# A new order for the first part of a decoder step, with four smaller edits in it

## The chip, the cores and the metric

The kernel runs on one core of one Trainium2 chip. The metric is the device time of one execution in microseconds (us). The profile describes one execution; the runs beside it are timed without it.

The engines are named as in the profile: PE (matrix engine), DVE (vector engine), ACT (scalar engine), POOL, and SP, which here only issues transfers (DMA). SBUF is the on-chip memory with 128 partitions, PSUM the small memory that PE writes into.

## What is computed

One layer of a decoder for 288 tokens: one prompt of 256, and 8 sequences with 4 new tokens each (the sample part, 32 tokens). Cut to what matters:

```python
z = rms_norm(x) @ w_in                      # 1024 -> u, va, q, k, vb, 512 each
u = gelu(u); va = rms_norm(gelu(va)); q = rms_norm(q); k = rms_norm(k)   # per head or group
# (A) gate, 4 groups of 128: within chunks of 128 tokens (prompt) or 4 (sample)
a = u * (tril(a_ws) @ va + a_bs)
# (B) attention, 8 heads of 64. Prompt: causal over 256 tokens. Sample: 8 pages of 128 past tokens
#     per sequence through a page table; of the four blocks of 256 past tokens a query keeps the
#     best three by q . mean(k), and always its own new tokens
o = softmax(q k^T / 8, selected) @ v
h = x + concat(a, o) @ w_out
h = h + relu(rms_norm(h) @ w_up)**2 @ w_down
h = h + ple_norm-scaled((sigmoid(rms_norm(h) @ w_ple_gate)) * (p @ w_ple_proj))
```

New k and v, and va of the sample part, are outputs too.

## The kernel before

Features lie on the partitions, tokens along the free dimension (N = 288). Every projection is done as high and low part: a weight chunk of 128 x 1024 (`raw`, 512 KB, four buffers) is split by ACT into `hi` (L124) and by DVE into `lo = raw - hi` (L129), three buffers each, and PE runs three matmuls for each 128 x 128 piece (`mm3`, L236 to L238). There are 98 such chunks, c0 to c97. A whole chunk is 24 matmuls of 288 columns. `split` (L242 to L246) makes the high and low part of an activation.

The first part, up to the output projection, is run by the string `ORDER`, one letter for a step; `w_up`, `w_down` and the last gate follow in loops. The letters: `r` first norm and the query projections c0 to c3 that are done beside it; `w` the next weight unit: key projections k0 to k3 (c4 to c7), values v0 to v3 (c8 to c11), the gate's va a0 to a3 (c12 to c15), u0 to u3 (c16 to c19), output projections out0.0 to out0.3 and out1.0 to out1.3; `E` one of the two chunks for the per-layer input (c24, c29); `T` the next tile of the page cache, K0 to K7 for keys, V8 to V15 for values, the first four of each for one half of the sequences, the last four for the other; `A` prompt attention for one pair of heads (A0 to A3); `G` the gate for one group (G0 to G3); `l` loads the gate's tables `aws`, `abd`, `abs` on ACT's queue, `m` masks them on DVE; `P` loads the per-layer input `pT` on ACT's queue; `s`, `S` store outputs. A unit is a generator: it issues its PE work at its place, and hands on the rest (`yield`) to be resumed some steps later.

PE and SP run in the order in which the program is written. ACT and DVE instructions are placed by a scheduler that looks at what each waits for. So what a PE step waits for depends on where its ACT and DVE steps came to stand.

PSUM: three buffers `mm` (projections), three `misc` (norm statistics, transposes, prompt scores, gates, new keys' scores, own values), two `S` (page scores and the weighted sum of values). Each prompt attention takes two `misc` buffers for its scores, each gate one.

A key tile (`u_K`, L556) is 16 matmuls of 32 query columns by 256 keys in four column tiles of the array. After the fourth tile of a half come the scores of the new keys (L564): four matmuls of 128 x 32 into `po`. DVE then works out which blocks each query keeps (L573 to L591), and ACT the exponentials (L594, L596). They are transposed into `PT`, and `u_V` multiplies: first the new values (L628), then eight matmuls of 512 columns for each value tile (L635). When the fourth value tile is in, DVE masks the sum per head (`Om`), and four matmuls with the constant `sel` (L650) bring the own value of each head into rows of features.

The statistic of a norm is a matmul with a block of ones (`stat`, L227 as `misc<-tmp`), then `rsqrt_act` (ACT: L256 reciprocal root y, L257 -x/2, L258 y squared) and `rsqrt_dve` (DVE: L262, L263), which is a Newton step.

Transfers: the 16 first-part tiles T are 8 pages of 256 KB each, issued by SP into four buffers, in order. Chunks c6 to c31 (`W_POOL` = 32) are issued from POOL's queue, all others by SP in line with the pages. The semaphores of transfers from SP's and ACT's queues are eight, taken in turn; a page whose turn comes on one that an earlier ACT transfer holds waits until that has landed.

Of the kernel before, what the change touches and what calls it, by code (L numbers as in the profile page):

```python
# [10 lines left out]
AF = mybir.ActivationFunctionType  # L11
# [14 lines left out]
NWARM = 8  # L26
NV = 38
NPOOL = 80
W_POOL = 32

ORDER = (
    "r w w w l w T w w T w w T w T w T w w m w T w w T w T A G T A G G T G s A A w T T P w T T w w T T S E w w w w E"
).split()

PLE = [4 + i for i, t in enumerate([t for t in ORDER if t in "wE"]) if t == "E"]
# [3 lines left out]
def tile_decode_step(ctx: ExitStack, tc: tile.TileContext, w, xT, pT, kT, vP, pt, const, aws, abd, abs_,  # L42
# [29 lines left out]
    pt_sb = stile([1, 64], "pt", dt=I32)  # L72
    cst = stile([128, 732], "const")
    aws_sb = stile([128, 4, 128], "aws")
    abd_sb = stile([NS, 4, NS], "abd")
    abs_sb = stile([128, 4, 128], "abs")

    gx = stile([128, NV + 8 * N], "h")
    vec_sb = gx[:, :NV]
    h = gx[:, NV:].rearrange("p (k n) -> p k n", k=8)  # L80
    ones = stile([128, 128], "ones")
    eps = stile([128, 1], "eps")
    pool.dma_start(pt_sb, pt)
# [37 lines left out]
    def split_hi(c, a=0, b=1024):  # L121
        if a == 0:
            hi[c] = stile([128, 1024], "hi", NHI, F32R)
        act.activation(hi[c][:, a:b], raw[c][:, a:b], AF.Copy)  # L124
# [105 lines left out]
    def tr(out, src, us=0.11):  # L230
        pe.transpose(out, src, ident)  # L231
        cur["pe"] += us
# [12 lines left out]
            act.activation(dh, src, AF.Copy, scale=scale)  # L245
            dve.scalar_tensor_tensor(dl, src, scale, dh.bitcast(F32), OP.mult, OP.subtract)  # L246

    def stat(src, lhsT):
        p = misc_ps()
        mm(p[:, :N], lhsT, src, 0.49, start=True, stop=True)  # L250
        return p[:, :N]

    def rsqrt_act(ss, count):

        y, v, y2 = tmp(), tmp(), tmp()
        act.activation(y, ss, AF.Abs_reciprocal_sqrt, bias=eps, scale=1.0 / count)  # L256
        act.activation(v, ss, AF.Identity, bias=heps, scale=-0.5 / count)  # L257
        act.activation(y2, y, AF.Square)  # L258
        return y, v, y2

    def rsqrt_dve(r, y, v, y2):
        dve.tensor_tensor(v, v, y2, OP.mult)  # L262
        dve.scalar_tensor_tensor(r, v, 1.5, y, OP.add, OP.mult)  # L263

    def g_rstd(name, acc):
        t = rsqrt_act(stat(acc, ones), D)
        yield 0
        st[name] = stile([128, N], "rs", 2)
        rsqrt_dve(st[name], *t)
# [15 lines left out]
    act.dma_start(gx[:, 0:NV + N], xT[:, 0:NV + N])  # L285
    load_x(act, 1, 2)
    first = stile([128, 1], "first")
    act.activation(first, eps, AF.Abs_reciprocal_sqrt)
    for c in range(1, 4):
        load_x(sp, 2 * c, 2 * c + 2)  # L290
        load_w(c, 2)
# [88 lines left out]
    def u_qk(c, name, tag, g):  # L380
        p = qp[c][:, :N] if c < 4 else k8(c, Ah, Al, misc_ps() if c == 5 else None)
        yield 1
        j, dst = in_tile(c, name, tag)
        dve.tensor_tensor(dst, p, st["r1"], OP.mult)
        sq = tmp()
        act.activation(sq, dst, AF.Square)
        yield (3.3 if c < 2 else 6.4 if c < 4 else 6,)
        t = rsqrt_act(stat(sq, blk), 64)
        yield 0
        r = tmp()  # L390
        rsqrt_dve(r, *t)
        dve.scalar_tensor_tensor(dst, dst, g, r, OP.mult, OP.mult)  # L392
        finish(name)
        if name == "q":
            for hh in range(2):
                pp = slice(64 * hh, 64 * hh + 64)
# [28 lines left out]
    def u_a(c):  # L425
        p = k8(c, Ah, Al)
        yield 1
        j, dst = in_tile(c, "a", "T1")
        dve.tensor_tensor(dst, p, st["r1"], OP.mult)
        act.activation(dst, dst, AF.Gelu_apprx_tanh)  # L430
        sq = early[:, 384 * j:384 * j + N]
        act.activation(sq, dst, AF.Square)
        st[f"sq{j}"] = sq
        if j < 3:
            return
        for i in range(2):
            yield (2.5,)
            ts = [rsqrt_act(stat(st[f"sq{j}"], ones), 128) for j in (2 * i, 2 * i + 1)]
            yield 0
            for j in (2 * i, 2 * i + 1):  # L440
                r = tmp()
                rsqrt_dve(r, *ts[j % 2])
                dst = st["a"][:, j]
                dve.scalar_tensor_tensor(dst, dst, avn(j), r, OP.mult, OP.mult)
        for j in range(4):
            if j % 2 == 0:
                yield (3.0,)
            t = early[:, 384 * j:384 * j + 384]
# [18 lines left out]
    def u_g(g):  # L467
        need(("u", 4), ("a", 4))
        an = st[f"an{g}"]
        p = misc_ps()  # L470
        cur["pe"] += 1.0
        for c in range(2):
            pe.matmul(p[:, 128 * c:128 * c + 128], lhsT=an[:, 128 * c:128 * c + 128], rhs=aws_sb[:, g, :],
                      start=True, stop=True)
        pe.matmul(p[:, NP:N], lhsT=an[0:NS, 256:384], rhs=abd_sb[:, g, :], start=True, stop=True)
        yield 1
        Mh, Ml = mix()
        t = tmp()
        dve.tensor_tensor(t[:, :NP].rearrange("p (c t) -> p c t", c=2), p[:, :NP].rearrange("p (c t) -> p c t", c=2),
                          abs_sb[:, g:g + 1, :].to_broadcast([128, 2, 128]), OP.add)  # L480
        dve.tensor_tensor(t[:, NP:].rearrange("p (b t) -> p b t", b=8), p[:, NP:N].rearrange("p (b t) -> p b t", b=8),
                          abs_sb[:, g:g + 1, 0:4].to_broadcast([128, 8, 4]), OP.add)
        dve.tensor_tensor(t, t, st["u"][:, g], OP.mult)
        act.activation(Mh[:, g], t, AF.Copy)
        yield 0
        dve.tensor_tensor(Ml[:, g], t, Mh[:, g].bitcast(F32), OP.subtract)
        finish("g")
# [57 lines left out]
    def u_K(t):  # L545
# [14 lines left out]
        if n == 3:  # L560
            need(("k", 4))
            po = misc_ps()
            for j in range(4):
                pe.matmul(po[:, 0:NS], lhsT=Qbd[:, 256 * j + 128 * g:256 * j + 128 * g + 128],  # L564
                          rhs=st["k"][:, j, NP:N], start=j == 0, stop=j == 3)
        cur["used"] += 1
        yield 1
        if n == 0:
# [51 lines left out]
    def u_V(t):  # L620
        g, n = t // 4 - 2, t % 4
        need((f"PT{g}", 1), ("v", 4))
        cur["pe"] += 1.9
        PT, vt = st[f"PT{g}"], kvt[t]
        if n == 0:
            st["O"] = s_ps()
            for b in range(4):
                pe.matmul(st["O"][32 * b:32 * b + 32, :], lhsT=PT[0:NS, 1024 + 32 * b:1056 + 32 * b], rhs=vn_s,  # L628
                          start=True, stop=False, tile_position=(0, 32 * b))
        O = st["O"]  # L630
        for j in range(2):
            for b in range(4):
                c = 128 * (2 * n + j) + 32 * b
                v0 = 512 * (2 * b + j)
                pe.matmul(O[32 * b:32 * b + 32, :], lhsT=PT[:, c:c + 32], rhs=vt[:, v0:v0 + 512],  # L635
                          start=False, stop=n == 3 and j == 1, tile_position=(0, 32 * b))
        cur["used"] += 1
        if n < 3:
            return
        finish(f"V{g}")  # L640
        yield 1
        Om = stile([128, 4 * N], "T4")[:, :512] if g else early[:, 0:512]
        dve.scalar_tensor_tensor(Om.rearrange("p (h d) -> p h d", h=8), O.rearrange("p (h d) -> p h d", h=8),
                                 st[f"rs{g}"], hmask[:, :, None].to_broadcast([128, 8, 64]), OP.mult, OP.mult)
        yield (1.6,)
        Mh, Ml = mix()
        p = misc_ps()
        cur["pe"] += 0.9
        for j in range(4):
            pe.matmul(p[:, 16 * j:16 * j + 16], lhsT=Om[:, 128 * j:128 * j + 128], rhs=sel, start=True, stop=True)  # L650
# [36 lines left out]

    def mask_aws():
        dve.tensor_tensor(aws_sb, aws_sb, tri[:, None, :].to_broadcast([128, 4, 128]), OP.mult)
# [211 lines left out]
```

## Time and profile before

| | us |
|---|---|
| median of 3 runs (lowest, highest) | 411.98 (411.09, 412.75) |
| profiled execution | 410.52 |
| its span in the profile | 408.8 |
| PE busy in it | 397.0 (97%) |
| DVE, ACT, POOL busy | 267.7, 211.1, 15.6 |
| mean granted clock of PE | 0.990 of full speed |

The span is what the profile's lines add up to; the execution is 1.7 us longer. A line of a timeline gives start, duration, engine, line of the code, operation, what it writes and reads, its shape, how many instructions of the kind stand together, and in brackets how long the engine was idle before and what ended that. Busy times of PE overlap a little, since its instructions are pipelined: the difference of two starts says better how long a group holds PE. In a list of waits stand the total, the number and the longest.

### The profile page before, as it was taken

The numbers are of one execution on the slowest core, as the hardware profiler recorded it, in microseconds if no ns is written. First come the engines' busy times: TensorE is split into PE (matmuls) and PEld (weight loads), VectorE is DVE, ScalarE is ACT, GpSimd is POOL, SyncE is SP. The second block draws the span as 40 slices with busy tenths as digits, with TensorE's granted clock in tenths as the row PEclk, the third lists the DMA queues.
The fourth block names the chain that finished last, engine by engine and source line by source line (L and its number), as shares of the span: only waits on it lengthen the run. The fifth ranks groups of instructions, "written<-read, shape, count | busy, mean of one in ns | idle before, by whom it ended". The sixth has DMA issues, their size and how long they took to land.

```text
span 408.8 us, 8115 instructions
## 1 busy us (share of the span) xinstructions
PE 397.0 (97%) x3082; PEld 364.0 (89%) x3082; DVE 267.7 (65%) x514; ACT 211.1 (52%) x377; POOL 15.6 (4%) x32
## 2 busy tenths in 40 slices
PE   8989999999799999999999999999999999999995
PEld 7978887987255679999999999999999999999994
DVE  4878765566587344969989778874454445544773
ACT  7677738588455225866554454444433343333630
POOL 1210110111000010000000000000000000000000
PEclk9999999999699999999999999999999999999999
DMA  8999899999949972444444454445444545444411
GB/s 283 402 396 353 311 398 393 391 391 388 372 132 313 396 283 101 156 162 179 176 156 156 164 179 173 156 156 170 180 163 157 162 170 185 154 157 171 154 54 49
DMA packets 37270, 92.39 MB, mean 226 GB/s; under 512 B 4656, under 2 KB 6096, under 8 KB 37232
## 3 DMA queue, kind: packets, MB, share of 16 engines
q1 hardware_dynamic: 32688, 77.10, 52.9%
q0 software_dynamic: 3776, 13.63, 8.7%
q10 hardware_dynamic: 768, 1.15, 0.9%
q8 instruction: 24, 0.39, 0.4%
q14 instruction: 14, 0.11, 0.1%
HBM read 89.44 MB, written 2.42 MB: 225 GB/s over the span
## 4 chain that ended last, share of the span: by engine, by line
PE 84%; DMA 5%; DVE 5%; ACT 3%; issue 2%; SPq 0%; DVEq 0%; POOLq 0%; ACTq 0%
PE mm L236 24%; PE mm L238 24%; PE mm L237 23%; PE S L635 4%; DMA raw<-w 3%; PE S L556 3%; PE misc L227 2%; PE misc L231 2%; DMA aws<-aws 1%; DVE lo L129 1%; DMA h<-xT 1%; ACT hi L124 1%; PE S L628 1%; DVE T L392 1%; DVE tmp L263 1%
## 5 line engine op out<-in xcount | busy, mean ns | idle before, releaser
L124 ACT ACTIVATE hi<-raw 128x1024 fp32r<-128x1024 f32 (+2 forms) x107 | 108.8, 1018 | 144.4 <-PE mm L237 123.2
L129 DVE TENSOR_TENSOR lo<-raw,hi 128x1024 fp32r<-128x1024 f32 (+2 forms) x107 | 125.4, 1173 | 64.0 <-ACT hi L124 62.2
L236 PE MATMUL mm<-T,hi 128*128 128x288 f32 x296 | 88.1, 298 | 0.0
L238 PE MATMUL mm<-T,lo 128*128 128x288 f32 x296 | 87.2, 294 | 0.0
L237 PE MATMUL mm<-T,hi 128*128 128x288 f32 x296 | 86.4, 292 | 0.0
L236 PE MATMUL mm<-Ah,hi 128*128 128x288 f32 x264 | 80.4, 305 | 0.0
L237 PE MATMUL mm<-Al,hi 128*128 128x288 f32 x264 | 77.9, 295 | 0.0
L238 PE MATMUL mm<-Ah,lo 128*128 128x288 f32 x264 | 77.7, 294 | 0.0
L236 PE MATMUL mm<-kv,hi 128*128 128x288 f32 x224 | 66.1, 295 | 0.0
L237 PE MATMUL mm<-kv,hi 128*128 128x288 f32 x224 | 66.0, 295 | 0.0
L238 PE MATMUL mm<-kv,lo 128*128 128x288 f32 x224 | 65.9, 294 | 0.0
L237 PEld LDWEIGHTS mm<-T,hi 128*128 128x128 f32 x296 | 55.7, 188 | 0.1
L236 PEld LDWEIGHTS mm<-T,hi 128*128 128x128 f32 x296 | 55.6, 188 | 0.1
L238 PEld LDWEIGHTS mm<-T,lo 128*128 128x128 f32 x296 | 55.4, 187 | 0.0
L236 PEld LDWEIGHTS mm<-Ah,hi 128*128 128x128 f32 x264 | 49.5, 188 | 2.8 <-issue 2.4
L237 PEld LDWEIGHTS mm<-Al,hi 128*128 128x128 f32 x264 | 49.6, 188 | 0.4
L238 PEld LDWEIGHTS mm<-Ah,lo 128*128 128x128 f32 x264 | 49.7, 188 | 0.0
L237 PEld LDWEIGHTS mm<-kv,hi 128*128 128x128 f32 x224 | 42.3, 189 | 0.0
L238 PEld LDWEIGHTS mm<-kv,lo 128*128 128x128 f32 x224 | 42.2, 189 | 0.0
L236 PEld LDWEIGHTS mm<-kv,hi 128*128 128x128 f32 x224 | 42.0, 188 | 0.0
L759 DVE TENSOR_TENSOR tmp<-mm,rs 128x288 f32<-128x288 f32 x32 | 14.6, 456 | 11.0 <-PE mm L238 10.9
L119 POOL DMA_DIRECT2D raw<-w x26 | 13.7, 529 | 143.6 <-DVE lo L129 143.6
(170 smaller groups left out, 432.9 us busy)
## 6 DMA issues: line engine op xcount, KB each, us to landing
raw<-w SPq DMA_DIRECT2D x72, 512.0 KB, 3.2
kv<-kT SPq DMA_DIRECT2D x64, 256.0 KB, 7.5
kv<-vP SPq DMA_DIRECT2D x64, 256.0 KB, 6.5
raw<-w POOLq DMA_DIRECT2D x26, 512.0 KB, 6.5
raw<-w SPq DMA_DIRECT2D x8, 256.0 KB, 4.9
y_o<-h SPq DMA_DIRECT2D x7, 144.0 KB, 1.8
h<-xT SPq DMA_DIRECT2D x3, 288.0 KB, 5.2
k_o<-T SPq DMA_DIRECT2D x1, 576.0 KB, 7.3
```

Source lines behind the costliest of these rows:

```text
L119: (pool if 6 <= c < W_POOL else sp).dma_start(raw[c][:, n * i:n * i + n], w[c][:, n * i:n * i + n])
L124: act.activation(hi[c][:, a:b], raw[c][:, a:b], AF.Copy)
L129: dve.tensor_tensor(lo[c][:, a:b], raw[c][:, a:b], hi[c][:, a:b].bitcast(F32), OP.subtract)
L227: pe.matmul(out, lhsT=lhsT, rhs=rhs, **kw)
L231: pe.transpose(out, src, ident)
L236: pe.matmul(out, lhsT=wh, rhs=xh, start=start, stop=False)
L237: pe.matmul(out, lhsT=wh, rhs=xl, start=False, stop=False)
L238: pe.matmul(out, lhsT=wl, rhs=xh, start=False, stop=stop)
L263: dve.scalar_tensor_tensor(r, v, 1.5, y, OP.add, OP.mult)
L556: pe.matmul(S[32 * b:32 * b + 32, c0:c0 + 256].rearrange("p (j s) -> p j s", j=2), lhsT=Qbd[:, q0:q0 + 32], rhs=kt[:, b, :, j, :], start=j ...
L635: pe.matmul(O[32 * b:32 * b + 32, :], lhsT=PT[:, c:c + 32], rhs=vt[:, v0:v0 + 512], start=False, stop=n == 3 and j == 1, tile_position=(0, ...
L759: dve.tensor_tensor(t, p, st["r2"], OP.mult)
```

## The change

It is five edits in one.

The order of the first part. With names in place of letters, before:

```
r k0 k1 k2 l k3 K0 v0 v1 K1 v2 v3 K2 a0 K3 a1 K4 a2 a3 m u0 K5 u1 u2 K6 u3 K7 A0 G0 V8 A1 G1 G2 V9 G3
s A2 A3 out0.0 V10 V11 P out0.1 V12 V13 out0.2 out0.3 V14 V15 S E(c24) out1.0-1.3 E(c29)
```

and after:

```
r k0 k1 k2 k3 v0 l v1 v2 K0 v3 a0 K1 K2 a1 m K3 a2 A0 K4 a3 u0 K5 K6 u1 u2 u3 K7 A1 G0 A2 G1 P G2 G3
V8 V9 A3 out0.0 V10 V11 out0.1 s V12 V13 out0.2 V14 out0.3 V15 S E(c24) out1.0-1.3 E(c29)
```

With it `W_POOL` goes from 32 to 26, so c26 to c31 are issued by SP: c26 behind V13's pages, the others behind V15's.

Shorter norms: for the first two model-wide norms and the four query norms the ACT step L257 goes, and the first of the two DVE steps now reads the statistic from PSUM; the model-wide norm's Square on ACT is put ahead of the split of c6 there. The fourth query statistic is written to an `S` buffer in place of `misc`. The new keys' scores become 16 matmuls of 32 x 32, in four column tiles. The own values become four transposes and a sum on DVE over 128 x 512 to 128 x 64. The gate's sample part multiplies over all 128 rows in place of 32, with `abd` padded by zeros from 16 to 64 KB and four POOL clears of 128 x 128.

```diff
-W_POOL = 32
+W_POOL = 26
 ORDER = (
-    "r w w w l w T w w T w w T w T w T w w m w T w w T w T A G T A G G T G s A A w T T P w T T w w T T S E w w w w E"
+    "r w w w w w l w w T w w T T w m T w A T w w T T w w w T A G A G P G G T T A w T T w s T T w T w T S E w w w w E"
...
-    abd_sb = stile([NS, 4, NS], "abd")
+    abd_sb = stile([128, 4, NS], "abd")
...
-        act.activation(hi[c][:, a:b], raw[c][:, a:b], AF.Copy)
+        i = act.activation(hi[c][:, a:b], raw[c][:, a:b], AF.Copy)
+        if c == 6:
+            after(i, st["r1_act"])
...
-    def rsqrt_act(ss, count):
+    def rsqrt_act(ss, count, short=False):
...
+        if short:
+            half, a = {1024: (1, 4), 64: (1, 2)}[count]
+            act.activation(y, ss, AF.Abs_reciprocal_sqrt, bias=eps[:, half:half + 1], scale=4.0 ** half / count)
+            st["r1_act"] = act.activation(y2, y, AF.Square, scale=2.0 ** -a)
+            dve.scalar_tensor_tensor(y2, ss, count * EPS, y2, OP.add, OP.mult)
+            return y, 1.5 * 2 ** half, y2
...
+        if isinstance(v, float):
+            dve.scalar_tensor_tensor(r, y2, v, y, OP.subtract, OP.mult, reverse0=True)
+            return
...
-        t = rsqrt_act(stat(acc, ones), D)
+        t = rsqrt_act(stat(acc, ones), D, True)
...
-        t = rsqrt_act(stat(sq, blk), 64)
+        t = rsqrt_act(stat(sq, blk, s_ps() if c == 3 else None), 64, c < 4)
...
+            pool.memset(t[:, 256:384], 0.0)
...
-        pe.matmul(p[:, NP:N], lhsT=an[0:NS, 256:384], rhs=abd_sb[:, g, :], start=True, stop=True)
+        pe.matmul(p[:, NP:N], lhsT=an[:, 256:384], rhs=abd_sb[:, g, :], start=True, stop=True)
...
-                pe.matmul(po[:, 0:NS], lhsT=Qbd[:, 256 * j + 128 * g:256 * j + 128 * g + 128],
-                          rhs=st["k"][:, j, NP:N], start=j == 0, stop=j == 3)
+                for b in range(4):
+                    q0 = 256 * j + 128 * g + 32 * b
+                    pe.matmul(po[32 * b:32 * b + 32, 0:NS], lhsT=Qbd[:, q0:q0 + 32], rhs=st["k"][:, j, NP:N],
+                              start=j == 0, stop=j == 3, tile_position=(0, 32 * b))
...
-            pe.matmul(p[:, 16 * j:16 * j + 16], lhsT=Om[:, 128 * j:128 * j + 128], rhs=sel, start=True, stop=True)
-        yield 1
+            tr(p[:, 128 * j:128 * j + 128], Om[:, 128 * j:128 * j + 128])
+        yield 1
+        o = tmp()[:, :64]
+        dve.tensor_reduce(o, p.rearrange("p (t h) -> p t h", h=8), AX.X, OP.add)
```

What moves on the engines, at two places. First DVE at the first norm. `lo_437` and `lo_436` are the low part of c5, `lo_439` and `lo_438` that of c6, `rs` the norm's scale, and the last row the first use of it. Before:

```order
27 L129 TENSOR_TENSOR lo_437<-raw_263,hi_395 128x1024
28 L129 TENSOR_TENSOR lo_439<-raw_265,hi_397 128x1024
29 L262 TENSOR_TENSOR tmp_383<-tmp_383,tmp_384 128x288
30 L263 SCALAR_TENSOR_TENSOR rs_388<-tmp_383,tmp_382 128x288
31 L384 TENSOR_TENSOR T_54_399<-S_111,rs_388 128x288
```

After:

```order
28 L137 TENSOR_TENSOR lo_436<-raw_264,hi_394 128x1024
29 L269 SCALAR_TENSOR_TENSOR tmp_384<-misc_381,tmp_384 128x288
30 L278 SCALAR_TENSOR_TENSOR rs_388<-tmp_384,tmp_383 128x288
31 L137 TENSOR_TENSOR lo_438<-raw_266,hi_396 128x1024
32 L402 TENSOR_TENSOR T_53_398<-S_112,rs_388 128x288
```

The norm's two steps now stand between c5's and c6's low parts, no longer behind both.

Second PE from key tile K7 (first row of each) to value tile V8 (last). L564 and L585 are the new keys' scores; L227 and L235 with `T,T` operands the scores of a prompt attention (A0 before; A1, then A2 after); L473, L475 and L492, L494 a gate; L628 and L649 the new values. Before:

```order
522 L556 MATMUL S_1435<-kv_1027,T_11_75 32x256 x16
523 L564 MATMUL misc_1560<-T_66_449,T_11_75 128x32 x4
524 L227 MATMUL misc_1596<-T_66_449,T_54_399 128x128
525 L227 MATMUL misc_1597<-T_66_449,T_54_399 128x128
526 L227 MATMUL misc_1596<-T_66_449,T_54_399 128x256
527 L227 MATMUL misc_1597<-T_66_449,T_54_399 128x256
528 L473 MATMUL misc_1618<-aws_63,e_74 128x128 x2
529 L475 MATMUL misc_1618<-abd_64,e_74 128x32
530 L628 MATMUL S_1634<-vns_379,PT_1198 32x512 x4
531 L635 MATMUL S_1634<-kv_1112,PT_1198 32x512 x8
```

After, from the end of G0 (rows 532 to 538 are the same steps as 522 to 528 before, for A1 and with 16 matmuls at L585):

```order
539 L494 MATMUL misc_1680<-abd_64,e_75 128x32
540 L235 MATMUL misc_1694<-T_65_448,T_53_398 128x128
541 L235 MATMUL misc_1695<-T_65_448,T_53_398 128x128
542 L235 MATMUL misc_1694<-T_65_448,T_53_398 128x256
543 L235 MATMUL misc_1695<-T_65_448,T_53_398 128x256
544 L492 MATMUL misc_1714<-aws_63,e_75 128x128 x2
545 L494 MATMUL misc_1714<-abd_64,e_75 128x32
546 L492 MATMUL misc_1734<-aws_63,e_75 128x128 x2
547 L494 MATMUL misc_1734<-abd_64,e_75 128x32
548 L492 MATMUL misc_1744<-aws_63,e_75 128x128 x2
549 L494 MATMUL misc_1744<-abd_64,e_75 128x32
550 L649 MATMUL S_1754<-vns_380,PT_1227 32x512 x4
```

Four more steps, A2 and three gates, now stand between G0 and the first value matmuls; A0 has gone ahead of K7.

More of the change, by code (lines that the diff above doesn't have):

```diff
@@ L81, in tile_decode_step @@
     ones = stile([128, 128], "ones")
-    eps = stile([128, 1], "eps")
+    eps = stile([128, 2], "eps")
     pool.dma_start(pt_sb, pt)
     dve.memset(ones, 1.0)
-    dve.memset(eps, EPS)
+    dve.memset(eps[:, 0:1], EPS)
+    dve.memset(eps[:, 1:2], 4 * EPS)
     heps = stile([128, 1], "heps")
@@ L123, in split_hi, with after @@
             hi[c] = stile([128, 1024], "hi", NHI, F32R)
-        act.activation(hi[c][:, a:b], raw[c][:, a:b], AF.Copy)
+        i = act.activation(hi[c][:, a:b], raw[c][:, a:b], AF.Copy)
+        if c == 6:
+            after(i, st["r1_act"])
+    def after(late, early):
+        tc.add_manual_dep(late.ins, early.ins.name, mybir.DependencyInfo(
+            mybir.DependencyClass.NoSync, mybir.DependencyReason.DATA), reason="after")
     def split_lo(c, a=0, b=1024):
@@ L246, in split, with stat @@
             dve.scalar_tensor_tensor(dl, src, scale, dh.bitcast(F32), OP.mult, OP.subtract)
-    def stat(src, lhsT):
-        p = misc_ps()
+    def stat(src, lhsT, p=None):
+        p = misc_ps() if p is None else p
         mm(p[:, :N], lhsT, src, 0.49, start=True, stop=True)
         return p[:, :N]
-    def rsqrt_act(ss, count):
-        y, v, y2 = tmp(), tmp(), tmp()
-        act.activation(y, ss, AF.Abs_reciprocal_sqrt, bias=eps, scale=1.0 / count)
+    def rsqrt_act(ss, count, short=False):
+        y, v, y2 = tmp(), None if short else tmp(), tmp()
+        if short:
[4 more added lines that the diff above has]
+            return y, 1.5 * 2 ** half, y2
+        act.activation(y, ss, AF.Abs_reciprocal_sqrt, bias=eps[:, 0:1], scale=1.0 / count)
         act.activation(v, ss, AF.Identity, bias=heps, scale=-0.5 / count)
@@ L287, in tile_decode_step @@
     first = stile([128, 1], "first")
-    act.activation(first, eps, AF.Abs_reciprocal_sqrt)
+    act.activation(first, eps[:, 0:1], AF.Abs_reciprocal_sqrt)
     for c in range(1, 4):
@@ L647, in u_V @@
         p = misc_ps()
-        cur["pe"] += 0.9
         for j in range(4):
-            pe.matmul(p[:, 16 * j:16 * j + 16], lhsT=Om[:, 128 * j:128 * j + 128], rhs=sel, start=True, stop=True)
+            tr(p[:, 128 * j:128 * j + 128], Om[:, 128 * j:128 * j + 128])
         yield 1
+        o = tmp()[:, :64]
+        dve.tensor_reduce(o, p.rearrange("p (t h) -> p t h", h=8), AX.X, OP.add)
         tk = slice(NP + 16 * g, NP + 16 * g + 16)
-        split(Mh[:, 4:8, tk], Ml[:, 4:8, tk], p[:, 0:64].rearrange("p (j t) -> p j t", j=4))
+        split(Mh[:, 4:8, tk], Ml[:, 4:8, tk], o.rearrange("p (j t) -> p j t", j=4))
         finish("O")
@@ L689, in mask_aws @@
         dve.tensor_tensor(aws_sb, aws_sb, tri[:, None, :].to_broadcast([128, 4, 128]), OP.mult)
-        dve.tensor_tensor(abd_sb, abd_sb, tri[0:NS, None, 0:NS].to_broadcast([NS, 4, NS]), OP.mult)
+        dve.tensor_tensor(abd_sb, abd_sb, tri[:, None, 0:NS].to_broadcast([128, 4, NS]), OP.mult)
     in_units = (
@@ L883 @@
         "pt": A(page_table).reshape(1, 64), "const": _constants(),
-        "aws": aws, "abd": abd.reshape(NS, 4, NS), "abs": A(a_bs)[0],
+        "aws": aws, "abd": np.concatenate([abd.reshape(NS, 4, NS), np.zeros((96, 4, NS), np.float32)]), "abs": A(a_bs)[0],
     }
```

## The prediction

> **What bounds the kernel now.** I read the page first, then windows cut at the places the change touches, then waits, timelines and the chain there.
>
> ```profile
> span 408.8 us, 8115 instructions
> PE 84%; DMA 5%; DVE 5%; ACT 3%; issue 2%; SPq 0%; DVEq 0%; POOLq 0%; ACTq 0%
> ```
>
> PE is the bound: the chain of work that ended last is 84% PE, the rest scattered. The granted clock dips once. So a change is worth what it takes out of PE's work or gaps. Windows (window, length, busy PE, PEld, DVE, ACT, POOL, granted clock, DMA share, GB/s):
>
> ```profile
> 30.00:99.95 69.95, 69.66 (x652) 59.52 (x650) 46.65 (x98) 49.81 (x100) 7.38 (x14) 1.00 1.01 375
> 99.95:105.03 5.08, 2.91 (x27) 2.30 (x23) 4.05 (x24) 2.05 (x6) 0.53 (x1) 0.88 1.05 392
> 105.03:110.60 5.57, 5.57 (x26) 0.93 (x26) 1.88 (x8) 3.23 (x15) 0.00 (x0) 0.50 1.03 387
> 110.60:121.60 11.00, 10.24 (x78) 6.33 (x78) 8.40 (x37) 5.03 (x18) 0.00 (x0) 1.00 0.48 164
> 121.60:152.97 31.37, 31.33 (x256) 20.35 (x254) 16.65 (x42) 10.46 (x25) 2.11 (x4) 1.00 0.90 325
> 180.00:260.00 80.00, 80.00 (x605) 79.89 (x604) 70.12 (x123) 40.90 (x63) 0.00 (x0) 1.00 0.47 164
> ```
>
> 99.95 is the end of key tile K7 and 152.97 the start of chunk c24: 53.0 us with a hole, a stretch at half clock (5.57 us at 0.50, and 0.12 x 5.08 / 0.5 = 1.2 us before it) and small waits. From there on PE streams without a gap, as in the last row: what is won earlier is not taken back.
>
> **Part by part.** *Short norms, c6's order, fourth statistic in another PSUM tag.*
>
> ```profile
> 19.09 0.65 PE L227 MATMUL misc<-tmp,ones 128*128 128x288 f32 x2
> 21.06 1.06 ACT L124 ACTIVATE hi<-raw 128x1024 fp32r<-128x1024 f32 x1 [4.02 <-DMA raw<-w]
> 22.15 1.23 DVE L129 TENSOR_TENSOR lo<-raw,hi 128x1024 fp32r<-128x1024 f32 x1 [3.34 <-ACT hi L124]
> 24.27 0.82 DVE L384 TENSOR_TENSOR T<-S,rs 128x288 f32<-128x288 f32 x2
> 27.33 0.45 DVE L384 TENSOR_TENSOR T<-misc,rs 128x288 f32<-128x288 f32 x1
> 25.97 1.33 PE L227 MATMUL misc<-tmp,const 128*128 128x288 f32 x4
> 29.59 0.75 PE L227 MATMUL misc<-tmp,const 128*128 128x288 f32 x2 [0.94 <-ACT tmp L257]
> 29.97 0.51 PE L236 MATMUL mm<-Ah,hi 128*128 128x288 f32 x1
> ```
>
> r1's statistic is done by 19.7, yet its ACT and DVE steps stand behind c6's halves, and ACT sits idle 4.02 us for c6. After, the norm goes first and is done in that idle time; the first L384 (L402 in after) then waits for lo(c6) alone, 22.15 + 1.23 = 23.38, against 24.27. Five such scalings at 0.41, lo(c7) at 1.23 and one more scaling, k1's, end at 23.38 + 2.05 + 1.23 + 0.41 = 27.1 (27.75 before). That frees the third statistic's buffer; the fourth now needs neither that nor the dropped ACT step (L257). Two records take 29.97 - 29.59 = 0.38, so both are in by 27.1 + 0.76 and k2 starts at 27.85, not 29.97: **-2.1**. Most: eight records packed, 25.97 + 4 x 0.38 = 27.5, -2.5. Least: only the 0.65 by which k1's scaling is earlier.
>
> *Order up to K7.* A0 goes ahead of K7 and two pairs of key tiles become adjacent.
>
> ```profile
> 92.23 1.86 PE S L556 x32
> 139.30 3.57 PE S L635 x32
> 38.12 4.73 DMA aws<-aws
> 42.87 0.69 DVE L689 TENSOR_TENSOR aws<-aws,const 128x512 f32<-128x512 f32 x1 [2.12 <-DMA aws<-aws]
> ```
>
> A tile alone takes 1.86, two neighbours 3.57 (value tiles): 2 x 0.15 = **-0.3** (0 to -0.6). The load of the gate's tables is issued one unit later against PE's rows. DVE stands at the mask L689 until its table lands (2.12 us now), and behind it on DVE are copies that value unit v2's transposes wait for: **+0.3** (0 to +1.0, half of that wait). The three loads also hold ACT's queue and, by shared semaphores, SP's pages for a while; PE's 69.66 busy of 69.95 in this window says that nobody on PE waits for those. A0 itself moves some 2.4 us of PE work (scores, transposes and values of a pair, 0.91 + 0.71 + 0.8 by rows further down) ahead of K7, worth nothing alone.
>
> *New keys' scores and gate.*
>
> ```profile
> 100.02 1.01 PE misc L564 x8
> 110.46 0.97 PE L227 MATMUL misc<-T,T 64*128 64x128 f32 x8
> 111.37 0.71 PE L473 MATMUL misc<-aws,e 128*128 128x128 f32 x4
> 112.01 0.40 PE L475 MATMUL misc<-abd,e 32*128 32x32 f32 x2
> 112.34 0.71 PE L473 MATMUL misc<-aws,e 128*128 128x128 f32 x4
> ```
>
> L564 holds PE 1.01 us, twice (K3, K7). After: 16 column-tiled matmuls, 32 columns each. A key tile has 16 of the same form with 256 columns in 1.86: that is the upper end (+0.85). Scaled by columns, 1.86 / 8 = 0.23, is the lower (-0.78). I take 0.6: eight groups of four that run side by side, each at half of what one 32-row record of L475 (below) holds PE, 0.165 with its change of form. So -0.4 each, **-0.8**. The Trainium skill speaks against this edit: "TensorEngine Tiling (Array Packing)", Instruction Overhead, gives each matmul some 60 cycles whatever its width; on that page's figure 32 records at 2.4 GHz would take 0.8 us, an estimate, and the gain would be 0.2 each. No row here has so small a column tile.
>
> L475's 32-row form takes 0.33 for two records, the 128-row L473 0.64 for four, 0.16 each, with four times the columns. With all rows two small records take at most 0.16: 4 x 0.17 = -0.7, and no change of form after it, which I add as -0.1: **-0.8** (0 to -1.1). Its costs are off PE: four POOL clears (POOL is nearly empty) and a table of 64 KB for 16 KB on ACT's queue.
>
> *Own values.*
>
> ```profile
> 133.96 1.06 PE misc L650 x8
> 154.83 0.80 PE misc L650 x8
> 115.17 0.87 PE L231 MATMUL misc<-const,PP 128*128 128x128 f32 x6
> 115.88 0.61 PE L473 MATMUL misc<-aws,e 128*128 128x128 f32 x4
> 133.75 0.69 DVE L611 COPY PT<-misc 128x512 f32<-128x512 f32 x1 [0.17 <-PE misc L231]
> ```
>
> Six transposes are issued in 115.88 - 115.17 = 0.71, so four take 0.47 for 0.80 to 1.06: **-0.7** for both. The new DVE sum over 128x512 is priced by the copy, 0.69, before the split into high and low parts. Its cover is the rest of c24 on PE, 24 matmuls at 80.00 / 605 = 0.132: 152.97 + 3.2 + 0.8 = 157.0, 1.4 us after the group's end at 155.6, of which the splits take about half now. So 0, or +0.7 if DVE is busy then.
>
> *The gate stretch.* After K7, PE now has A1, G0, A2, G1, G2, G3, then V8, in place of A1, G0, V8.
>
> ```profile
> 103.96 0.47 ACT L594 ACTIVATE T<-S,b 128x256 f32<-128x256 f32 x1 [3.03 <-DVE b L591]
> 105.03 1.93 PE L628 MATMUL S<-vns,PT 32*32 32x512 f32 x8 [2.17 <-ACT T L594]
> 106.89 3.64 PE L635 MATMUL S<-kv,PT 128*32 128x512 f32 x16
> 116.76 0.48 PE L227 MATMUL misc<-T,T 64*128 64x128 f32 x2
> 118.35 1.17 PE L231 MATMUL misc<-const,e 128*128 128x128 f32 x6
> 119.94 0.87 PE L227 MATMUL misc<-PPT,vnp 128*64 128x256 f32 x8 [0.42 <-DVE pmx L508]
> 138.31 0.99 PE S L628 x8
> ```
>
> V8's first matmuls (L628) waited 2.17 for the selection's exponentials, 5.08 after K7. Now the work ahead of V8 is about 0.6 + 2 x 0.9 + 4 x 0.75 = 5.4 us, more than that wait, so it goes: -2.17. But three misc buffers serve all six steps: A2's scores need both of A1's, which DVE frees only after its maxima (four, 101.91 to 103.38 in the trace, between the selection's own small steps), and G2 needs one of A2's. Walking it by those durations, PE idles 0.7 before A2 and 0.65 before G2, and V8 starts 6.7 after K7. A3 waits 0.45 similarly. **+1.8** (0.5 to 3). Without the half clock L628 takes 0.99, not 1.86, and a value tile 1.86, not 3.57: **-2.6**. The small waits go because A2's exponentials now end long before its transposes: scores at 116.76 held 118.35 - 116.76 = 1.59 against 111.37 - 110.46 = 0.91 at full pace, transposes 119.94 - 118.35 = 1.59 against 0.71: **-1.6**.
>
> Sum: -2.1 - 0.3 + 0.3 - 0.8 - 0.8 - 0.7 - 2.17 + 1.8 - 2.6 - 1.6 = **-9.0**, on a profiled execution of 410.52 (span 408.8 and 1.7 around it): 401.5. The median of the runs is 411.98, 1.46 above that execution, so 403.0.
>
> **Is the data there?** SP's pages and weights must come 9 us earlier.
>
> ```profile
> SPq L143 <- DMA T<-pT: 7.7, 1, 7.7
> 118.46 0.33 ACTq L329 DMA_DIRECT2D T<-pT  x1
> DMA to landing us min/median/max: 2.7/2.7/2.7
> ```
>
> From 110.60 to 152.97 the windows moved 11.0 us at 164 and 31.4 at 325 GB/s = 12.0 MB, which at 387 GB/s needs 31 us of 42.4: 11 spare, against 9 taken. The low share at 110.6 is SP itself: one of its pages shares a semaphore with ACT's load of pT and stood 7.7 us until that landed. After, pT is issued behind A2's exponentials in ACT's queue and once G3's product has read u, whose place it takes: by my walk 9.7 after K7 (7.9 for G3's product), near 109. It lands at 111.7; the stream stands from about 103 until then. Some 36 pages and c26 (now on SP, behind V13's pages) remain at 256 KB / 387 = 0.66: V15 lands near 141, PE wants it near 142. Covered, with about 1 us to spare. Chunks c27 to c31 move from POOL's queue to SP's, behind the last page; they are wanted after c25, one per 3.2 us, while DMA runs at 164 GB/s: nothing, and the 3 MB leave the crowded stretch.
>
> **Rivals.** (1) *The clock halves again.* Before, it halved with PE idle for 2.17 us and busy 2.91 of 5.08 just ahead. After, the same place has 5.4 busy of 6.7: better, but in small records with gaps. If it halves for the same 6.8 us, PE loses up to 3.4; with 3.0, 406.0. A gap of 2.17 was enough before; two of about 0.7 are less, so somewhat under a quarter. The Trainium skill, "TensorE: Matmul & The Clock Gate", What's actually happening, has the clock drop after an idle window of about 3.4 us: by that it would drop in neither kernel, and the trace of before, with half clock after 2.17 idle, does not agree.
> (2) *Pages late.* If pT issues 3 us later than walked, or the lane blocks earlier, V14 and V15 wait 1 to 3 us: 405.0. For it: the spare is 1 us. Against: no wait of PE for pages in the trace of before.
> (3) *No change*: both together, A1's and G1's waits at their upper end (+1.2) and L564 losing 0.85 twice (+2.5 against the sum): 403 + 3.0 + 2.0 + 3.7 = 411.7.
> (4) *Slower*: the pT wait alone. V15's landing moves one for one with pT's. It decides at 1 + 9 + 2 = 12 us later than walked, pT issued near 121, that is, if ACT reached it only after A3's exponentials, as it was before relative to the gate (118.46). Then 414 and above. ACT's order after has A2's exponentials, then pT, then A3's, which speaks against.
>
> **How the numbers follow.** Within 0.5% is 409.9 to 414.0, about what the runs tell apart. Forecast 0.51 (own range 400 to 405), (1) 0.22, (2) 0.12, (3) 0.09, (4) 0.06. Faster 0.85, same 0.09, slower 0.06. The range takes in the forecast, (1) and (2), 400 at the low end (norms -2.5, new idle 0.5, gate -1.1 together give 401.0, and 1 for the tiles and scores), 408.5 at the high end ((1) at 3.4 with (2) at 2).
>
> **What would show it.** Right: k2 starts near 27.9 with no wait for an ACT step of the statistics; no 0.5 clock after 20 us; no wait of L649 on an exponential; V8 about 6.7 us after K7; K7's end to c24's start about 44.5 us; the new-key group about 0.6. Wrong: SP waiting for pT beyond V8's start with PE waiting at L656 for kv; PE idling on DVE's maxima for more than 3 us in the gate; a wait of out1's first matmuls on the DVE sum.

## The result, and the profile after

The changed kernel takes 400.59 us (median of 4 runs, 399.58 to 400.78) against 411.68 (411.09 to 412.75): a ratio of 0.9727, 95% interval 0.9692 to 0.9763. It is 11.1 us faster; 9.0 were forecast, for a time of 403.0. The profiled executions stand at 400.78 and 410.52, 9.7 apart.

Two windows of the changed kernel that answer to the five of before (length, busy PE, PEld, DVE, ACT, POOL, granted clock, DMA share, GB/s):

```profile
100.30:106.52 6.22, 5.75 (x77) 4.61 (x69) 5.97 (x37) 3.41 (x16) 0.00 (x0) 1.00 1.00 371
106.52:144.06 37.54, 37.29 (x305) 21.99 (x304) 21.74 (x60) 13.97 (x38) 0.00 (x0) 1.00 0.94 333
```

K7's end, 100.30, to V8's start is 6.22 with PE busy 5.75; V8 to c24's start is 37.54 with PE busy 37.29, all at full clock. Together 43.8, where before had 53.0. On PE's timeline the stretch reads:

```profile
98.55 1.93 PE L575 MATMUL S<-kv,T 128*32 128x256 f32 x32
100.30 0.48 PE L585 MATMUL misc<-T,T 128*32 128x32 f32 x32
100.71 0.93 PE L235 MATMUL misc<-T,T 64*128 64x128 f32 x8
...
102.68 0.49 PE L235 MATMUL misc<-T,T 64*128 64x128 f32 x2 [0.26 <-DVE pmx L527]
103.38 0.92 PE L235 MATMUL misc<-T,T 64*128 64x128 f32 x6 [0.21 <-DVE pmx L527]
...
106.52 1.06 PE L649 MATMUL S<-vns,PT 32*32 32x512 f32 x8
107.51 3.64 PE L656 MATMUL S<-kv,PT 128*32 128x512 f32 x32
111.08 0.87 PE L239 MATMUL misc<-const,e 128*128 128x128 f32 x6
```

The new keys' 32 small records hold PE 100.71 - 100.30 = 0.41, where eight held it 1.01. A2's scores (102.68) wait for DVE's maxima (L527) twice. V8 (L649) waits for nothing and takes 0.99 to its first tile; the two tiles behind it take 111.08 - 107.51 = 3.57, as one did at half clock.

The norm region, and the two new waits that came behind it:

```profile
26.17 1.62 PE L235 MATMUL misc<-tmp,const 128*128 128x288 f32 x6
27.63 0.65 PE L235 MATMUL S<-tmp,const 128*128 128x288 f32 x2
27.90 0.51 PE L244 MATMUL mm<-Ah,hi 128*128 128x288 f32 x1
47.31 0.52 PE L239 MATMUL misc<-const,T 128*128 128x128 f32 x3 [0.80 <-DVE T L437]
50.47 0.52 PE L239 MATMUL misc<-const,T 128*128 128x128 f32 x3 [0.74 <-DVE T L437]
```

k2 starts at 27.90 with no wait among the statistics. But the transposes of the values, at 47.31 and at 50.47 behind K0, wait 0.80 and 0.74 for copies on DVE. The profiled execution of before had one such wait of 0.29, behind K1:

```profile
49.61 0.52 PE L231 MATMUL misc<-const,T 128*128 128x128 f32 x3 [0.29 <-DVE T L419]
```

DVE's timeline in the changed kernel says why:

```profile
43.64 0.69 DVE L711 TENSOR_TENSOR aws<-aws,const 128x512 f32<-128x512 f32 x1 [2.68 <-DMA aws<-aws]
45.00 0.29 DVE L712 TENSOR_TENSOR abd<-abd,const 128x128 f32<-128x128 f32 x1 [0.67 <-DMA abd<-abd]
```

DVE stands 2.68 for the table aws and 0.67 for abd, and has its splits, norms and copies still to do.

### The profile page after: what moved, and what is told of

The parts are those of the page before. It is cut to its first block, busy times and chain, and to the rows that moved or that the text cites. A ratio compares the mean times of both kernels' runs of the same rounds, so it can differ in the third digit from the quotient of the medians.

```text
span 399.0 us, 8187 instructions
## 1 busy us (share of the span) xinstructions
PE 389.8 (98%) x3122; PEld 362.1 (91%) x3122; DVE 267.8 (67%) x517; ACT 208.8 (52%) x370; POOL 13.3 (3%) x30
## 4 chain that ended last, share of the span: by engine, by line
PE 90%; DVE 4%; DMA 3%; ACT 2%; issue 1%; DVEq 0%; POOLq 0%; ACTq 0%
PE mm L244 25%; PE mm L245 25%; PE mm L246 25%; PE S L656 4%; PE S L575 3%; PE misc L235 3%; PE misc L239 2%; DMA abd<-abd 2%; DMA pt<-pt 1%; DVE lo L137 1%; PE S L245 1%; PE S L246 1%; PE misc L244 1%; PE misc L245 1%; PE misc L246 0%
## 5 line engine op out<-in xcount | busy, mean ns | idle before, releaser
L783 ACT ACTIVATE kv<-tmp 128x288 fp32r<-128x288 f32 x28 | 12.4, 442 | 6.9 <-DVE tmp L782 6.7
```

Of the source, the lines that this page charges most:

```text
L783: act.activation(hid[m][:, 0], r, AF.Copy)
```

## Experiments

The runs are compared with the kernel before on the same chip. Where less than one us matters, their traces are read, since runs of one kernel lie up to 3 us apart.

**The order alone (e1), and the edits alone (e2).** The kernel before with the new `ORDER` and `W_POOL`, and the changed kernel with the old ones.

```diff
# order alone, in the kernel before
-W_POOL = 32
+W_POOL = 26
-    "r w w w l w T w w T w w T w T w T w w m w T w w T w T A G T A G G T G s A A w T T P w T T w w T T S E w w w w E"
+    "r w w w w w l w w T w w T T w m T w A T w w T T w w w T A G A G P G G T T A w T T w s T T w T w T S E w w w w E"
# edits alone, in the changed kernel: the same two in reverse
```

> The kernel before with only the new ORDER and W_POOL = 26; the four edits are left out. Theory A (the gain is two halves that add): the new order takes out the wait at V8 (2.2), the half clock (2.6) and the small waits of A3's scores and transposes (1.6), and pays about 1.1 of new idle in the gates and about 1.2 for the later table load: near 408, 3.8 under before, no half clock. Theory B (the order carries nearly all, the edits only shift idle time): near 402. Theory C (the edits carry it): above 410, half clock still there.

> The changed kernel with the old ORDER and W_POOL = 32; all four edits stay. Theory A: the edits are worth 5.4 where PE has no wait behind them (norms 2.1, new keys 1.3, gate 1.1, own values 0.9), but the part ahead of V8 (0.6 of the new keys, 0.3 of G0) only lengthens V8's wait for the exponentials, from 2.2 to about 3: near 407.3, half clock still there. Theory B: near 411. Theory C: near 402, and no half clock.

Order alone 404.0 (403.9 to 404.1), ratio 0.9816 (0.9789 to 0.9844), 7.9 under before. Edits alone 407.6 (405.0 to 408.5), ratio 0.9883 (0.9839 to 0.9927), 4.3 under. They add to 12.2, with 11.1 for both together: no large part of either needs the other. Theory A's number for the edits holds (407.3), that for the order (408) does not: it was worth twice as much. It had charged the order with 1.2 for the late table, and this kernel does not pay that: with the long norms in front, PE reaches the transposes after the copies are done. The kernel before does pay there in its second trace (last experiment), 0.30 and 0.84. From the new keys' scores behind K7 to c24 the order alone takes 45.3 in place of 53.0; less the 2.3 of A0's work that went ahead of K7 that is a gain of 5.4, about the 5.3 that theory A has for this part. Edits alone, PE after K7:

```profile
100.44 0.48 PE L585 MATMUL misc<-T,T 128*32 128x32 f32 x32
104.71 1.06 PE L649 MATMUL S<-vns,PT 32*32 32x512 f32 x8 [2.14 <-ACT T L615]
105.89:109.30 3.41, 3.41 (x18) 0.60 (x10) 1.87 (x8) 2.05 (x9) 0.00 (x0) 0.50 1.04 395
```

The half clock stays (3.4 us in this execution), and so does V8's wait, 2.14. It did not grow to 3 as expected: V8 starts 4.3 after the new keys' scores begin, where it was 5.1 before. The likely reason is that the shorter scores bring DVE's chain, and with it the exponentials, forward by about as much as they free on PE.

**V8 back between G0 and A2 (e3).**

```diff
-    "... w w w T A G A G P G G T T A ..."
+    "... w w w T A G T A G P G G T A ..."
```

> The changed kernel with V8 put back between G0 and A2 (K7 A1 G0 V8 A2 G1 P G2 G3 V9). Theory A: V8 waits about 2.7 for the exponentials with PE busy less than half of the windows before it, the granted clock halves for one or two of its windows as before: 3 to 5 slower than the changed kernel, 403.6 to 405.6. Rival (the clock drops only after a whole window of about 3.4 us without work): the clock stays 1.0 and only the wait less the saved idle of the gates is paid: 1.0 to 2.0 slower.

405.4 (404.9 to 406.6), ratio 0.9847 (0.9817 to 0.9876): 4.8 over the changed kernel's 400.6. Theory A. Two windows, cut where the clock changes, and the wait:

```profile
105.13 1.56 PE L649 MATMUL S<-vns,PT 32*32 32x512 f32 x8 [2.15 <-ACT T L615]
102.14:105.55 3.41, 1.25 (x12) 0.87 (x14) 2.79 (x19) 1.50 (x7) 0.00 (x0) 1.00 1.01 377
105.55:112.38 6.83, 6.83 (x35) 2.13 (x28) 2.37 (x11) 2.81 (x13) 0.00 (x0) 0.50 0.88 318
```

One step moved brings back the wait of 2.15 and 6.83 us at half clock, twice 3.41. So the place of V8 against the gates holds most of what the order won. The rival that the clock needs a whole window without work does not hold here: PE was busy 1.25 of the 3.41 before, and its longest wait there was 2.15.

**The long norms in the changed kernel (e4).**

```diff
-        if c == 6:
-            after(i, st["r1_act"])
-        t = rsqrt_act(stat(acc, ones), D, True)
+        t = rsqrt_act(stat(acc, ones), D)
-        t = rsqrt_act(stat(sq, blk, s_ps() if c == 3 else None), 64, c < 4)
+        t = rsqrt_act(stat(sq, blk), 64)
```

> The changed kernel with the long norms, c6's split in the scheduler's place and the fourth query statistic back in misc. Theory A: k2 starts 2.1 later and all after it moves one for one: 402.7. Rival: the wait of v2's and K0's transposes behind the gate's table (1.5 in the changed kernel) is set by the load's landing, and takes up part of it: only 0.6 to 1.2 slower.

401.8 (401.0 to 402.6), ratio 0.9757 (0.9728 to 0.9786), an interval that overlaps the changed kernel's. The trace decides for the rival. It is set beside the kernel with V8 early, which has the short norms and the same program up to there, and started as late (27.6):

```profile
27.59 1.62 PE L235 MATMUL misc<-tmp,const 128*128 128x288 f32 x6
29.05 0.65 PE L235 MATMUL S<-tmp,const 128*128 128x288 f32 x2
51.02 0.52 PE L239 MATMUL misc<-const,T 128*128 128x128 f32 x3 [0.77 <-DVE T L437]
```

```profile
27.67 1.62 PE L233 MATMUL misc<-tmp,const 128*128 128x288 f32 x6
29.95 0.75 PE L233 MATMUL misc<-tmp,const 128*128 128x288 f32 x2 [0.67 <-ACT tmp L270]
51.08 0.55 PE L237 MATMUL misc<-const,T 128*128 128x128 f32 x3
```

From the first statistic to the transposes behind K0 both take 23.4. The short norms (first rows) are 0.9 ahead at the last statistic, and the wait for the copies takes it back. DVE's mask of aws starts at 44.95 and 44.94 in the two, whatever the norms did. The medians, 1.2 apart, lie at the upper end of what the rival gave, and do not tell the two apart.

**The masks held back (e5).** DVE's two masks may only follow the first half's key tiles, so that DVE does not stand for the tables; then the same with the long norms (e6).

```diff
+        st["kred"] = dve.tensor_reduce(bs[:, n:n + 1], S[:, c0:c0 + 256], AX.X, OP.add)
...
-        dve.tensor_tensor(aws_sb, aws_sb, tri[:, None, :].to_broadcast([128, 4, 128]), OP.mult)
+        after(dve.tensor_tensor(aws_sb, aws_sb, tri[:, None, :].to_broadcast([128, 4, 128]), OP.mult), st["kred"])
# the same for abd_sb; "m" five steps later in ORDER
```

> The changed kernel with the two masks of the gate's tables (L711, L712) held back on DVE until after the K tiles of the first half; PE's order is the same. Theory D (from the runs so far): K0's transposes came at 50.4 to 51.1 in five kernels, whatever the norms did, because DVE stands at the mask until the table lands (42.9 to 45.0); so the norms' 2.1 were mostly given back there. Then DVE runs on, the 1.5 of waits at v2 and K0 go, and it is 1.0 to 1.7 faster than the changed kernel: 399.0. Rival (the copies are late for another reason, the splits and Newton steps DVE has to do there anyway): within 0.4 of the changed kernel, 400.6.

> e5 with the long norms, c6's split in the scheduler's place and the fourth statistic in misc. Theory D: with the mask out of the way nothing gives the norms' gain back: 0.9 to 2.2 slower than e5, by how early PE's start stands against c6's landing. Rival (the norms buy nothing at all): within 0.4 of e5.

```profile
28.94 0.65 PE L235 MATMUL S<-tmp,const 128*128 128x288 f32 x2
49.95 0.55 PE L239 MATMUL misc<-const,T 128*128 128x128 f32 x3
```

```profile
29.71 0.75 PE L233 MATMUL misc<-tmp,const 128*128 128x288 f32 x2 [0.67 <-ACT tmp L270]
50.83 0.55 PE L237 MATMUL misc<-const,T 128*128 128x128 f32 x3
```

With the masks late (first pair) both waits are gone and K0's transposes come at 49.95; with the long norms as well (second pair) at 50.83, 0.9 later, and the medians are 400.15 (398.8 to 400.4) and 401.23 (401.1 to 401.3), 1.1 apart. So theory D: it was the table's landing that gave the norms' gain back, and without that wait they are worth about 1 in these two traces, whose statistics both start late, at 27.4 to 27.5. As a whole the late masks are not shown to help: 0.9733 (0.9696 to 0.9771) against the changed kernel's 0.9727, where 1.0 to 1.7 us were expected. At K0's transposes they are 1.1 ahead of the kernel with V8 early, which starts as late (49.95 to 51.02); why the medians do not show it stays open.

**Two small edits undone (e7, e8).**

```diff
# new keys: four 128 x 32 matmuls again
+                pe.matmul(po[:, 0:NS], lhsT=Qbd[:, 256 * j + 128 * g:256 * j + 128 * g + 128],
+                          rhs=st["k"][:, j, NP:N], start=j == 0, stop=j == 3)
# gate: 32 rows again; table and clears stay
-        pe.matmul(p[:, NP:N], lhsT=an[:, 256:384], rhs=abd_sb[:, g, :], start=True, stop=True)
+        pe.matmul(p[:, NP:N], lhsT=an[0:NS, 256:384], rhs=abd_sb[0:NS, g, :], start=True, stop=True)
```

> The changed kernel with the new keys' scores as four 128 x 32 matmuls again. By the trace of after the group takes 0.41 for 1.01, and the key tile ahead of it 1.75 for 1.86: 0.6 to 0.7 each at K3 and K7 if PE is what counts, 1.3 slower, 401.9. Rival (behind K7 the gates wait for DVE's maxima anyway): only K3's 0.6, 401.2, with K7 to V8 as long as now (6.2).

> The changed kernel with the gate's sample part over 32 rows again; table and POOL clears stay. Four gates at 0.14 to 0.29 go back to 0.33 each and their first matmuls from 0.55 to 0.64: 0.9 slower at most, 401.5. Rival: G0 to G3 wait for misc buffers and DVE's maxima, the time from K7 to V8 stays near 6.2 and less than 0.4 is lost.

401.9 (two runs, 401.6 and 402.2) and 401.5 (401.3 and 401.6). K7's end and V8's start with the old keys, then with the old gate:

```profile
100.60 1.08 PE L583 MATMUL misc<-T,T 128*128 128x32 f32 x8
107.35 1.06 PE L647 MATMUL S<-vns,PT 32*32 32x512 f32 x8
```

```profile
100.57 0.48 PE L585 MATMUL misc<-T,T 128*32 128x32 f32 x32
107.42 1.06 PE L649 MATMUL S<-vns,PT 32*32 32x512 f32 x8
```

6.75 and 6.85 in place of 6.22: 0.53 of the keys' 0.60 and 0.63 of the gates' 0.9 reach V8, the rest falls into the waits for DVE's maxima. Neither rival holds: the idle time in this stretch hides little of what is added. Two runs each are too few to price the edits by their medians.

**pT's load later (e9).** `P` behind V11 and out0.1.

```diff
-    "... T A G A G P G G T T A w T T w s ..."
+    "... T A G A G G G T T A w T T w P s ..."
```

> The changed kernel with step P four steps later (behind V11 and out0.1), so that ACT issues pT's load between A1's two copies, about 3.7 later after K7 than now (8.1). In the changed kernel V15's last page lands at 142.1 and PE starts V15 at 142.2. Theory E (the page stream has no spare left): V15 and V14 come 2.5 to 3.7 later and PE waits for them: 403 to 404. Rival (the waits of SP are taken up by the free buffers, pages are wanted later than tile starts say): within 0.6 of the changed kernel.

402.2 (402.1 to 403.4), ratio 0.9778 (0.9757 to 0.9800), 1.7 over the changed kernel. SP now waits 8.5 for pT, in place of 5.4, and PE waits in the value tiles. First the changed kernel's V14, which V15 equals there, then this kernel's V14 and V15:

```profile
136.96 1.92 PE L656 MATMUL S<-kv,PT 128*32 128x512 f32 x16
```

```profile
SPq L151 <- DMA T<-pT: 8.5, 1, 8.5
137.44 1.16 PE L656 MATMUL S<-kv,PT 128*32 128x512 f32 x6
138.91 1.90 PE L656 MATMUL S<-kv,PT 128*32 128x512 f32 x10 [0.30 <-DMA kv<-vP]
144.12 2.68 PE L656 MATMUL S<-kv,PT 128*32 128x512 f32 x16
```

V14 takes 3.30 to the next unit and V15 2.61, not 1.85: 2.2 more for 3.1 more of waiting on SP. So about 0.9 was the spare; the forecast had 1. It is theory E's mechanism, at less than its price.

**pT's load from POOL's queue (e10), and A1 ahead of K7 as well (e11).** Both with the late masks.

```diff
-        act.dma_start(p_sb, pT)
+        pool.dma_start(p_sb, pT)
# second kernel, also:
-    "... m w T T w w w T A G A G P G G T T A ..."
+    "... m w T T w A w w T G A G P G G T T A ..."
```

> e5 (late masks) with pT's load issued from POOL's queue in place of ACT's, so that none of SP's pages shares its semaphore. SP's 5.4 of waiting for pT go and V15 lands 3 to 5 earlier against K7. Theory E: in e5 the pages were only just in time, PE does not wait for them, so the time stays: within 0.4 of e5, 400.1. Rival (pages already held e5 back): 0.5 to 1.0 faster, 399.3.

> e10 with A1 moved ahead of K7 (between u1 and u2; after K7: A1's transposes, G0, A2, G1, A1's values, G2, G3). DVE then has no maxima of A1 between K7 and V8. Expected if misc buffers and DVE's maxima make the 1.1 of idle left between K7 and V8: G0 and A2 no longer wait, K7 to V8 falls from 6.2 to about 5.7 with A1's transposes and values in it, A3's wait of 0.4 stays: 1.0 to 1.5 faster than e10, 398.8. Rival (DVE's chain of the selection is the limit, about 4.7 from K7 to its exponentials, and A1 ahead of K7 only delays u2 and u3): same as e10.

406.15 (402.3 to 407.0), ratio 0.9881 (0.9851 to 0.9912), and 402.6 (401.4 to 403.2), 0.9785 (0.9756 to 0.9815): the first slower than the changed kernel, the second not clearly so, and both against both theories. SP no longer waits for pT, and issues its last page at 131.9 instead of 136.8 in the changed kernel. But with pT on another queue, ACT's split of pT (L250) came to stand ahead of its copies of A1's transposes (L548):

```profile
112.04 0.68 ACT L250 ACTIVATE T<-T 128x576 fp32r<-128x576 f32 x1 [1.89 <-DMA T<-pT]
```

```profile
113.16 0.55 PE L239 MATMUL misc<-const,PP 128*128 128x128 f32 x3 [1.28 <-ACT PPT L548]
```

ACT (first fence) waits 1.89 for pT, PE (second) 1.28 for ACT. The traced execution, 402.3, lies 2 over that of e5, and these waits account for most of it. The other three, 405.3 to 407.0, show a mean clock of 0.988 to 0.992 against 0.995, so half clock is the likely rest; no trace here shows where. With A1 early, K7 to V8 takes 107.59 - 100.30 = 7.3: A2's scores wait 0.62 for the selection's steps on DVE. No version here is shown to beat the changed kernel.

**The kernel before once more (e12)**, for a second trace.

> The kernel before once more, for a second trace. The runs of before span 409.5 to 412.8 and the profiled one was at the low end (410.5). Theory F (where the 1.2 come from that the forecast carried over and that the changed kernel does not have): PE's clock comes up 1.6 later in some executions, the norm region then starts near 27.6 in place of 26.0, and before has no later wait that takes it up fully, while the changed kernel does, at the gate's table. Then a trace that starts late has K7's end 0.9 or more later than 99.95. Rival: the half-clock stretch is longer in the slower executions.

411.8, span 410.1, 1.3 above the first trace. The window 8 to 11 us of the first trace, then of this one with rows of its timelines and one more window:

```profile
8.00:11.00 3.00, 3.00 (x24) 3.00 (x24) 3.00 (x7) 3.00 (x7) 0.00 (x0) 1.00 1.03 376
```

```profile
8.00:11.00 3.00, 3.00 (x19) 3.00 (x19) 3.00 (x6) 3.00 (x8) 0.00 (x0) 1.00 1.01 369
27.42 1.62 PE L227 MATMUL misc<-tmp,const 128*128 128x288 f32 x6
30.14 0.51 PE L236 MATMUL mm<-Ah,hi 128*128 128x288 f32 x1
44.09 0.69 DVE L689 TENSOR_TENSOR aws<-aws,const 128x512 f32<-128x512 f32 x1 [3.14 <-DMA aws<-aws]
50.83 0.52 PE L231 MATMUL misc<-const,T 128*128 128x128 f32 x3 [0.84 <-DVE T L419]
101.17 1.08 PE L564 MATMUL misc<-T,T 128*128 128x32 f32 x8
105.24:112.06 6.82, 5.81 (x26) 1.17 (x28) 2.40 (x10) 4.24 (x19) 0.00 (x0) 0.50 1.05 393
```

PE is as busy and gets 19 matmuls done instead of 24: they start 0.24 apart up to 9.67 and 0.13 apart after that. The column of the clock says 1.00 throughout; it is the starts that show the late rise. The statistics start 1.45 later, at 27.42, and K7 ends 1.22 later, at 101.17. The half clock is 6.82, as long as before, so the rival does not hold. Theory F's number came out, but its path did not. At k2 only 0.17 is left of the 1.45 (30.14 after 29.97), because the last statistic waits there in both traces (0.94 in the first, 0.74 in this one). The 1.22 come at the table: the mask starts at 44.09 after 42.87, as its load took 5.8 in place of 4.7, and PE passes the transposes behind K1 at 50.83 after 49.61. Ahead of K1 they wait 0.30 as well. So the kernel before has that wait too. Whether the late rise has to do with the longer load is not shown.

## Why the prediction was right, and where it was off

The direction, the place and the main mechanism were right, and 400.59 lies inside the range, near its low end. By its own terms, found in the profiled executions:

| term | forecast | found |
|---|---|---|
| norms, to k2 | -2.1 | -2.07 (29.97 to 27.90); not kept |
| neighbouring key tiles, two pairs | -0.3 | -0.3 (3.59 for 2 x 1.86, twice) |
| table for the gate | +0.3 | +1.25 (0.80 + 0.74, less 0.29); +0.4 against the second trace of before (less 1.14) |
| new keys' scores, both | -0.8 | -1.3 (1.01 to 0.41, and 0.1 off the key tile ahead) |
| gate's sample part | -0.8 | -1.0 by starts; 0.6 of it reach V8 |
| own values | -0.7 | -1.0 (0.92 and 0.81 to 0.41 and 0.35, by starts) |
| V8's wait | -2.17 | gone |
| idle in the gates | +1.8 | +1.6 |
| half clock | -2.6 | gone |
| A3's small waits | -1.6 | gone |

The rows found add to 9.2 of the 9.7; the other 0.5 are in no row.

- The gate stretch came out almost as walked: V8 6.2 after K7 (6.7 forecast), K7 to c24 43.8 (44.5). The two runs that move only this stretch, order alone and V8 early, confirm that the wait and the half clock are the core.
- The term that failed is the table's load. The forecast took it for a cost of its own with at most +1.0 and let the norms' -2.1 stand beside it. In fact they are two ends of one thing: PE cannot pass the values' transposes before the table has landed and DVE has caught up, so what the norms win ahead of it is handed back. The pairs with early and late masks show it, and the traces agree on when PE gets through. In both traces of before it passes the transposes behind K1 6.74 after the mask begins (42.87 to 49.61, 44.09 to 50.83). With V8 early, the old gate and pT late it passes those behind K0 6.07 after it (44.95 to 51.02, 44.67 to 50.74, 44.78 to 50.85). With the old order and the short norms the two waits are 0.54 and 0.85, so the norms' gain is lost there as well.
- New keys: the price was taken at 0.6 between 0.23 and 1.86; it is 0.41. The estimate by the Trainium skill ("TensorEngine Tiling (Array Packing)", Instruction Overhead), 0.8 for 32 records at some 60 cycles each, is twice that. The code has 16 matmuls there, two records each; counted by these, the same figure gives 0.4, an estimate too. Which count is the right one no run here decides.
- The own values' DVE sum cost nothing on PE: no wait stands at out1's first matmuls, as forecast.
- The step from the profiled execution to the median was wrong: 1.46 were added to both kernels. In the result the median of before lies 1.16 above its profiled execution, and that of the changed kernel 0.19 below its own. That is about 1.35 of the 2.1 between 11.1 and 9.0; the other 0.74 lie between the two profiled executions. The second trace of before shows how such a slower execution comes about: the table lands later, and K7 ends 1.22 later. In the changed kernel's three traces that start late (27.4 to 27.6, in the runs with V8 early, the old gate and pT late) K0's transposes are only 0.3 to 0.6 later than its own, 50.74 to 51.02. That the untraced executions differ by the same wait is likely and not shown.
- That the number lies in the range is in part luck. Of the norms' 2.1, the largest early gain of the sum, 1.25 went at the table in the profiled execution and all of it in the pair of e4; what made up for it were smaller edits worth more than forecast and a step to the median that the forecast had wrong.
- Rival (1), half clock again, did not come in the changed kernel, but one step less between K7 and V8 brings it. Rival (2), pages late, stood 0.9 us away. V15's landing near 141 does not follow from the terms given for it (111.7 and 38 times 0.66 make 136.8); the last page was issued at 136.8 and landed about 142.1, so near the forecast by luck. Rivals (3) and (4) did not come; the mechanism of (4), pT's load holding SP, costs 0.7 for each us of waiting on SP by the run with P late.

## What to carry to other kernels

Work that does not depend on a late result, put ahead of the first step that needs it, can save that step's wait and also the clock that the wait costs. Before a gain early in a kernel is added to others, look for the next place where the engine waits for a transfer: a gain ahead of it is returned there. And a load moved to another queue can move the instructions that use it too; look at what then stands behind its first reader.

## What the runs showed of the hardware

The granted clock halved for 3.4 or 6.8 us after a stretch in which PE was partly busy. These are the 3.41 us ahead of the change of clock in before, in its second trace and with the edits alone, then the emptiest such stretch behind K7 in the changed kernel, with no change after it, and last one ahead of K7 in before, again with no change after it:

```profile
100.36:103.77 3.41, 2.50 (x20) 1.89 (x19) 2.88 (x20) 0.57 (x1) 0.53 (x1) 1.00 1.05 391
101.83:105.24 3.41, 2.25 (x18) 1.65 (x17) 2.88 (x21) 0.39 (x2) 0.29 (x1) 1.00 1.02 377
102.48:105.89 3.41, 1.27 (x13) 0.31 (x16) 2.07 (x13) 2.26 (x11) 0.00 (x0) 1.00 1.03 388
100.78:104.20 3.42, 2.95 (x22) 2.01 (x22) 3.35 (x23) 0.70 (x3) 0.00 (x0) 1.00 1.02 382
28.68:32.09 3.41, 2.50 (x17) 2.39 (x18) 2.53 (x5) 2.63 (x8) 0.53 (x1) 1.00 1.05 393
```

In the first four rows, busy 2.50 and less was followed by half clock, and 2.95 was not (nor 3.25, the emptiest behind K7 in the order alone). But the fifth is as empty as the first, and in the traced run with pT on POOL's queue a stretch of 2.14 (109.92 to 113.34) was not followed by half clock either, so busy time alone does not settle it. The Trainium skill, "TensorE: Matmul & The Clock Gate", What's actually happening, has the clock set by free-running windows of some 3.4 us, and halved after an idle one. The half clock of 3.41, 6.82 and 6.83 us agrees with such windows; that a whole idle window is needed these traces contradict, as PE was busy 1.25 to 2.50 in the stretch ahead of each drop behind K7.
